# Griffin block on one core: the sums of w_o's blocks and of two of the values' weights made by accumulating DMAs

## The chip, the cores and the metric

The kernel runs on one core of one Trainium2 chip. The metric is the device time of one execution in microseconds (us). All data are float32.

## The reference

One layer of a streaming encoder for 512 rows of width 1024: a norm, one combined projection, two branches (attention over chunks, and a gated recurrence), a merge with two gates, the product with w_o, and a gated feed-forward block.

```python
xn = rmsnorm(x, norm_mix_g)
q, k, v, xr, gr, ga, gb = split(xn @ w_in)
ya = chunked_band_attention(q, k, v, rel_table) @ w_attn_out
hr = rg_lru(causal_depthwise_conv(xr, conv_w, conv_b), ...)
yb = (hr * gelu(gr)) @ w_rnn_out
h = x + (sigmoid(ga + b_a) * ya + sigmoid(gb + b_b) * yb) @ w_o
g, up = split(rmsnorm(h, norm_ffn_g) @ w_ffn_in)
out = rmsnorm(h + (silu(g) * up) @ w_ffn_out, final_norm_g)
```

## The kernel before

**Split products.** Every operand of a large product stands as a high part in the reduced format fp32r and a low part, the rest. ScalarE (ACT) makes the high part with a copy, VectorE (DVE) the low part with a difference (`split`, L84 to L87; in the profile L86 is the high part, L87 the low one). TensorE (PE) then makes three matmuls for each 128 rows of depth (`mm3`, L80 to L82). The tiles of the two parts are called `whl_...`, the loaded weights `raw_...`. Raw weights go through a ring of three buffers of 128x1024 that all stages share, so that a load waits until the tile three loads before it has been split.

**Seven products.** The values (`v_`), the merge with w_o (`o_`) and the feed-forward units (`fg0`, `fu0`, `fg1`, ...) are computed with seven block products in place of eight. Each needs the weight's blocks w11, w21, w22 and four sums of blocks, t1 to t4. On the other side stand sums of the rows' blocks, s1 to s4 (for the values made in `x_sums`, L966). A product of the values or of w_o is 24 matmuls of 512 columns.

**Who makes the sums before.**
- For w_o and for the first feed-forward weights (`f_`), `sums_kept` (L321) loads four blocks of one half of the depth, makes t1 to t4 with four DVE differences of 128x1024, and stores them in DRAM: t1 and t2 of w_o raw, t3 and t4 of w_o already split, as pairs of 1 MB. It runs at the end of the recurrence's loop steps j = 2, 4 (w_o), 6 (f), and once more behind the first key tile (f).
- For the values, `v_weight_sums` (L287) loads three blocks for each half of the depth and makes t1 and t2 with two DVE differences, at j = 3 and 5 of the products with w_rnn_out (`po_yb`), which stand just ahead of the values' products. t3 and t4 are made from t2 as they are needed.
- For w_ffn_out, accumulating DMAs make them: SyncE (SP) copies a block in DRAM (`out_copy`, L222), and later GpSimd (POOL) issues a DMA that adds a second block to it (`out_add`, L226). A small copy to a `cell` makes POOL wait for a given point first. Copies go in each of the 16 heads of the attention, adds behind heads 9, 11, 13 and 15, in the products with w_attn_out (`po_ya`), and in units fg1 and fg2.

**The order.** PE's order is written out by hand from the values on. DVE, ACT, POOL and SP take their instructions in the order that a scheduler found, with some of them kept in the program's order. SP issues nearly all loads, one after the other; an instruction that waits holds up what stands behind it on its engine.

**The merge's stage.** `o_product` (L1222) runs w11, w21, t1, t2, w22, t3, and between the two halves of the second norm, t4. `weights(name, n)` makes ready the weights of the next n products. Behind t3, `norm_half` (L513) transposes the normed rows: a square with a row sum (`hj`), its total (`hsq`), a root (`sd_ffn`), a reciprocal (`rs_ffn`), the scaled rows (`xs_ffn`), then PE's transposes (`pt_ffn`). The feed-forward's first product, w11 of fg0, follows t4.

**The attention.** Each of the 16 heads has its score products on PE, `p` made by DVE and ACT, the scaling of `p` on POOL (L1091), transposes on PE, and the weighted values. In every head POOL also finishes a tile of biases that a DMA brings (L738).

## Time and profile before

| what | value |
|---|---|
| median of 3 runs | 847.2 us (847.09 to 848.59) |
| the profiled execution | 848.82 us |
| its span in the trace | 847.0 us |
| mean granted clock of TensorE | 0.997 |
| DMA traffic | 153.96 MB, mean 182 GB/s |

The span is the time from the first to the last recorded instruction. Times at the start of a row are us from the start of the span; the second number is the time that the row was busy. Brackets at the end of a row hold the idle time ahead of it and what ended that. Matmuls overlap, so PE's pace is read from the starts: at full rate a matmul of 512 columns starts every 0.227 us. The change's places in the span are the recurrence's loop (to about 190 us), the products with w_rnn_out (196 to 242), the values (242 to 282), the attention (282 to 425) and the merge with the start of the feed-forward block (468 to 520).

### The profile page before, as it was taken

The page shows a single profiled execution, that of the slowest core. Times are in us where ns is not written, and L with a number is a line of the kernel's source. Part 1 is how long each engine was busy: PE and PEld are TensorE (multiplying, and loading weights), DVE is VectorE, ACT ScalarE, POOL GpSimd, SP SyncE. Part 2 cuts the span into 40 slices and gives each one's busy share as a digit, 9 for nine tenths or more (in the row PEclk, how much of TensorE's full clock was granted, in tenths as well). Part 3 has the DMA queues.
Part 4 walks back from the last instruction along what each step waited for, and adds up shares of the span by engine and source line. Part 5 has one row for each costly group of instructions (what it writes and reads, how often), then busy time and mean ns, then how long its engine had stood idle before and what let it go on. Part 6 is the DMA issues. An engine that isn't in the chain of part 4 may idle for free.

```text
span 847.0 us, 11664 instructions
## 1 busy us (share of the span) xinstructions
PE 837.2 (99%) x4102; PEld 708.8 (84%) x4102; DVE 654.1 (77%) x960; ACT 524.3 (62%) x868; POOL 159.9 (19%) x207
## 2 busy tenths in 40 slices
PE   9999999999999999999999999999999999999996
PEld 6988888888878888888888888888888999988885
DVE  6667779886999778777568777889777878599784
ACT  7595848773456678878544469663765466555543
POOL 2412030221040043343211000005102322200000
PEclk9999999999999999999999999999999999999998
DMA  8433386687565444549448984555955576455442
GB/s 286 166 103 117 130 298 243 212 271 243 167 205 150 132 134 148 157 152 223 94 132 211 320 294 154 157 187 166 229 176 159 150 187 207 140 177 168 160 165 99
DMA packets 104058, 153.96 MB, mean 182 GB/s; under 512 B 8024, under 2 KB 62896, under 8 KB 103488
## 3 DMA queue, kind: packets, MB, share of 16 engines
q1 hardware_dynamic: 99040, 141.32, 51.2%
q0 software_dynamic: 3728, 8.96, 6.4%
q10 hardware_dynamic: 1232, 2.95, 0.9%
q8 instruction: 32, 0.52, 0.3%
q14 instruction: 26, 0.21, 0.1%
HBM read 139.53 MB, written 30.45 MB: 201 GB/s over the span
## 4 chain that ended last, share of the span: by engine, by line
PE 84%; DVE 7%; ACT 4%; DMA 3%; issue 2%; ACTq 0%; DVEq 0%
PE fu_x L80 2%; PE fu_x L81 2%; PE fu_x L82 2%; PE o L1122 2%; PE fg_x L82 2%; PE fg_x L80 2%; PE fg_x L81 2%; PE pT L1102 2%; PE po_ga L82 2%; PE po_ya L80 2%; PE po_ya L82 2%; PE p_out L81 2%; PE p_out L80 2%; PE po_ya L81 2%; PE p_out L82 2%
## 5 line engine op out<-in xcount | busy, mean ns | idle before, releaser
L1326 POOL TENSOR_TENSOR sg<-sg,keep_fu_x 128x512 f32<-128x512 f32 (+1 forms) x10 | 17.8, 1784 | 163.4 <-DVE keep_fu_x L1325 163.4
L1091 POOL TENSOR_SCALAR p<-p,rl 128x128 f32<-128x128 f32 (+3 forms) x61 | 43.8, 733 | 13.7 <-DVE rl L1087 9.4
L1085 DVE CUSTOM_DVE_ANT_0 p<-s,bias 128x128 f32<-128x128 f32 (+1 forms) x64 | 28.6, 486 | 12.6 <-PE s L1077 11.1
L1086 ACT ACTIVATE p<-p,m 128x128 f32<-128x128 f32 (+1 forms) x64 | 35.5, 555 | 2.3 <-DVE m L1085 2.0
L87 DVE TENSOR_TENSOR whl_fu_w<-raw_fu_w,whl_fu_w 128x1024 fp32r<-128x1024 f32 (+1 forms) x18 | 22.1, 1230 | 9.0 <-ACT whl_fu_w L86 9.0
L87 DVE TENSOR_TENSOR pp<-pT,pp 128x384 fp32r<-128x384 f32 (+1 forms) x48 | 26.9, 595 | 2.0 <-ACT pp L86 1.8
L81 PE MATMUL po_xr<-xnT,whl_xr 128*128 128x512 f32 (+1 forms) x80 | 27.7, 354 | 0.0
L87 DVE TENSOR_TENSOR whl_fu_t<-t_fu,whl_fu_t 128x1024 fp32r<-128x1024 f32 (+1 forms) x18 | 23.2, 1293 | 5.9 <-ACT whl_fu_t L86 5.7
L81 PE MATMUL po_gr<-xnT,whl_gr 128*128 128x512 f32 (+1 forms) x80 | 27.5, 347 | 0.0
L82 PE MATMUL po_gr<-xnT,whl_gr 128*128 128x512 f32 (+1 forms) x80 | 27.3, 347 | 0.0
L82 PE MATMUL po_xr<-xnT,whl_xr 128*128 128x512 f32 (+1 forms) x80 | 27.3, 347 | 0.0
L80 PE MATMUL po_gr<-xnT,whl_gr 128*128 128x512 f32 (+1 forms) x80 | 27.2, 347 | 0.0
L738 POOL MEMSET bias<- 64x64 f32 x16 | 2.5, 155 | 130.7 <-DMA bias<-ext_d 130.7
L80 PE MATMUL po_xr<-xnT,whl_xr 128*128 128x512 f32 (+1 forms) x80 | 26.3, 352 | 0.4 <-ACT xnT L649 0.4
L86 ACT ACTIVATE whl_fu_w<-raw_fu_w 128x1024 fp32r<-128x1024 f32 (+1 forms) x18 | 17.7, 987 | 13.0 <-issue 7.1
L80 PE MATMUL po_k<-xnT,whl_qk 128*128 128x512 f32 x64 | 25.5, 398 | 0.0
L80 PE MATMUL po_q<-xnT,whl_qk 128*128 128x512 f32 x64 | 25.5, 398 | 0.0
L80 PE MATMUL po_ga<-xnT,whl_ga 128*128 128x512 f32 x64 | 25.5, 398 | 0.0
L80 PE MATMUL po_gb<-xnT,whl_gb 128*128 128x512 f32 x64 | 25.3, 395 | 0.0
L86 ACT ACTIVATE whl_fu_t<-t_fu 128x1024 fp32r<-128x1024 f32 (+1 forms) x18 | 17.7, 989 | 12.2 <-PE fu_x L82 8.9
L82 PE MATMUL po_ga<-xnT,whl_ga 128*128 128x512 f32 x64 | 25.1, 392 | 0.1
L81 PE MATMUL po_q<-xnT,whl_qk 128*128 128x512 f32 x64 | 25.0, 390 | 0.0
(610 smaller groups left out, 3036.8 us busy)
## 6 DMA issues: line engine op xcount, KB each, us to landing
raw_qk<-in_w_in_dram SPq DMA_DIRECT2D x32, 256.0 KB, 3.3
out_t<-in_w_ffn_out_dram SPq DMA_DIRECT2D x16, 512.0 KB, 5.5
raw_fu_w<-in_w_ffn_in_dram SPq DMA_DIRECT2D x16, 512.0 KB, 4.7
raw_fo<-in_w_ffn_out_dram SPq DMA_DIRECT2D x14, 512.0 KB, 4.3
raw_t<-out_t SPq DMA_DIRECT2D x24, 256.0 KB, 3.3
raw_xr<-in_w_in_dram SPq DMA_DIRECT2D x8, 512.0 KB, 6.0
raw_gr<-in_w_in_dram SPq DMA_DIRECT2D x8, 512.0 KB, 4.5
raw_ga<-in_w_in_dram SPq DMA_DIRECT2D x8, 512.0 KB, 4.9
```

The costliest lines, as they stand in the source:

```text
L80: pe.matmul(o, sh, mh, start=start, stop=False, skip_group_check=parts)
L81: pe.matmul(o, sh, ml, start=False, stop=False, skip_group_check=parts)
L82: pe.matmul(o, sl, mh, start=False, stop=stop, skip_group_check=parts)
L86: act.activation(hi, src, AF.Copy)
L87: dve.tensor_sub(lo, src, f(hi))
L738: pool.memset(b[64:128, 448:512], NEG)
L1085: dve.tensor_tensor_reduce(prob[qb][:], scs[qb][:, 0:w], bias[:, S - w:S], -1.0, 3e38, ALU.add, ALU.min, nmax[:, qb:qb + 1])
L1086: act.activation(prob[qb][:], prob[qb][:], AF.Exp, bias=nmax[:, qb:qb + 1], scale=-1.0, accum_out=lsum[:, qb:qb + 1])
L1091: eng.tensor_scalar(prob[qb][:], prob[qb][:], rl[:, qb:qb + 1], 1.0, ALU.mult, ALU.mult)
L1102: pe.transpose(pt[:, at * P:(at + 1) * P], prob[qb][:, kb * P:(kb + 1) * P], ident[:])
L1122: pe.matmul(po[:, S - n:S], st, pp[i][:, part, lo:lo + n], start=kb == 0 and part == 0, stop=kb == NT - 1 and part == 1)
L1326: (pool if keep and (unit != f_units[-1] or side) else dve).tensor_mul(o, o, keep[a] if keep else banks[a])
```

## The change

1. t1 to t4 of w_o are made by eight copies in DRAM (SP, heads 0 to 7) and eight accumulating DMAs (POOL, heads 2 to 9). They stand in DRAM raw, so t3 and t4 are now loaded raw (four loads of 512 KB) and split by ACT and DVE, as t1 and t2 were. t3's weights are made ready one product ahead in place of two.
2. `sums_kept` runs for f alone, at j = 2 and 4.
3. t1 and t2 of the values are made by four copies (SP, behind j = 0) and six accumulating DMAs (POOL, four at j = 2 and two at j = 4, every second one behind a `cell`). t1 is loaded through a raw buffer, t2 into the tile that it had.
4. The accumulating DMAs only add, so the signs of some sums change, and with them the signs in `x_sums`, in the merge's row sums and in what is done with the products.
5. The low parts of f's w11 are kept in the program's order (`PINNED`).
6. The copies for w_ffn_out go in heads 8 to 15 and in units fu0 and fg1, their adds behind heads 11, 13, 14, 15, in the products with w_attn_out, and in fu1 and fg2.

```diff
-COPIES = [1] * 16
-ADDS_AT = (9, 11, 13, 15)
-ADDS = {"fg1": 1, "fg2": 1}
+PINNED = (("f", "w11", 0), ("f", "w11", 1))
+COPIES = [0] * 8 + [1] * 8
+ADDS_AT = (11, 13, 14, 15)
+ADDS = {"fu1": 1, "fg2": 1}
...
+    def v_copy(kind, n):
+
+        block = {"t1": (0, 1), "t2": (1, 1), "t3": (1, 1), "t4": (1, 0)}[kind]
+        tc.keep_in_program_order(sp.dma_start(out=v_t[kind, n][:], in_=v_rows(*block, n)))
+
+    def v_add(kind, n, k, after=None):
+
+        if after is not None:
+            cell = cp.tile([P, NT], F32, tag="lsum", bufs=2, name=f"cell_v{kind}{n}_{k.start}")
+            tc.keep_in_program_order(pool.tensor_copy(cell[:, 0:1], after))
+        one = v_t[kind, n][:]
+        two = v_rows(0, int(kind == "t3"), n) if kind in ("t1", "t3") else v_t["t1" if kind == "t2" else "t2", n][:]
+        tc.keep_in_program_order(pool.dma_start(out=one[:, k], in_=two[:, k], accum_op=ALU.add, max_dma_last_dim=4096))
...
-    def v_weight_sums(u):
-
-        b11, b12, b22 = v_raw("t", 0, 0, u), v_raw("t", 0, 1, u), v_raw("t", 1, 1, u)
-        t1, t2 = (aw.tile([P, 2, S], F32, tag="v", bufs=4, name=f"v_t{n}_{u}")[:] for n in (1, 2))
-        dve.tensor_sub(t1, b12, b11)
-        dve.tensor_sub(t2, b22, t1)
...
-            if kind == "t1":
-                src = v_t1[u]
-            elif kind in ("t2", "t4"):
+            if kind in ("t1", "t2"):
+                if kind == "t1":
+                    src = wp.tile([P, 2, S], F32, tag="raw", bufs=3, name=f"raw_v_{kind}_{u}")[:]
+                else:
+                    src = v_t2[u] = aw.tile([P, 2, S], F32, tag="v", bufs=4, name=f"v_t2_{u}")[:]
+                for n in range(2):
+                    sp.dma_start(out=src[:, :, n * CW:(n + 1) * CW], in_=v_t[kind, n][:, 2 * u:2 * u + 2])
+            elif kind == "t4":
                 src = v_t2[u]
...
+    def o_copy(kind, u):
+
+        block = {"t1": (0, 1), "t2": (1, 1), "t3": (1, 1), "t4": (1, 0)}[kind]
+        tc.keep_in_program_order(sp.dma_start(out=o_t[kind, u][:], in_=o_rows_of(*block, u)))
+
+    def o_dma_add(kind, u):
+
+        two = o_rows_of(0, int(kind == "t3"), u) if kind in ("t1", "t3") else o_t["t1" if kind == "t2" else "t2", u][:]
+        tc.keep_in_program_order(pool.dma_start(out=o_t[kind, u][:], in_=two, accum_op=ALU.add, max_dma_last_dim=4096))
...
-            split(hl[u][:, 0], hl[u][:, 1], raw[:])
+                sp.dma_start(out=raw[:], in_=o_t[kind, u][:] if w == "o" else kept_sums[w, int(kind[1])][u].rearrange("p (k e) -> p k e", k=2))
+            act.activation(hl[u][:, 0], raw[:], AF.Copy)
+            ins = dve.tensor_sub(hl[u][:, 1], raw[:], f(hl[u][:, 0]))
+            if (w, kind, u) in PINNED:
+                tc.keep_in_program_order(ins)
...
+                if j < 6:
+                    v_next()
+                    v_next(conv[j + c][2][:, 0:1])
...
+        for what in v_copies[:4] if not j else ():
+            v_copy(*v_copies.pop(0))
         if j:
-            sums_kept(obp, "oof"[j // 2 - 1], (0, 1, 0)[j // 2 - 1])
+            if j < 6:
+                sums_kept(obp, "f", j // 2 - 1)
...
-        if j in (3, 5):
-            v_weight_sums(j // 2 - 1)
...
+            if h < 8:
+                o_copy(*o_copies.pop(0))
             step(copies, COPIES[h])
-            if h in ADDS_AT:
+            if 2 <= h < 10:
+                o_dma_add(*o_adds.pop(0))
+            elif h in ADDS_AT:
                 step(adds)
...
-        w = weights(f"o_{kind}", 2)
+        w = weights(f"o_{kind}", 1 if kind in ("t3",) else 2)
...
+        if unit in f_units[1:3]:
+            step(copies, kind in after)
```

What moves on the engines is shown at three places. Line numbers are those of each kernel's own code.

The first is DVE ahead of the values' products, at the second head's scores (`p`, `m`). Before, the split of w11 (`whl_v_w`), of t1 (`whl_v_t`) and one of the row sums (`v_s`, L981):

```order
L1085 ISA p_2_2171,m_2167<-s_2_2174,bias_2163 128x384
L1085 ISA m_2167 128x1
L87 TENSOR_TENSOR whl_v_w_0_2198<-raw_v_w_000_2200,whl_v_w_0_2198 128x1024
L1085 ISA p_3_2172,m_2167<-s_3_2175,bias_2163 128x512
L1085 ISA m_2167 128x1
L87 TENSOR_TENSOR whl_v_w_1_2199<-raw_v_w_001_2205,whl_v_w_1_2199 128x1024
L981 TENSOR_TENSOR v_s_1897<-v_s_1897,xnT 128x1024
L1152 SCALAR_TENSOR_TENSOR zb_486<-zb_486,po_yb_2197 128x512
L1087 RECIPROCAL rl_2168<-l_2166 128x4
L87 TENSOR_TENSOR whl_v_t_0_2269<-v_t_0_2049,whl_v_t_0_2269 128x1024
```

Now, from a little earlier in the same stretch:

```order
L1032 TENSOR_TENSOR v_s_1877<-v_s_1877,xnT 128x1024
L1201 SCALAR_TENSOR_TENSOR zb_493<-zb_493,po_yb_2055 128x512
L1138 RECIPROCAL rl_2026<-l_2024 128x4
L88 TENSOR_TENSOR v_s4l<-v_s_1877,v_s4h 128x1024
L88 TENSOR_TENSOR whl_v_w_0_2152<-raw_v_w_000_2154,whl_v_w_0_2152 128x1024
L1201 SCALAR_TENSOR_TENSOR zb_493<-zb_493,po_yb_2091 128x512
L1136 ISA p_0_2123,m_2121<-s_01_2127,bias_2117 128x128
L1136 ISA m_2121 128x1
L1136 ISA p_1_2124,m_2121<-s_01_2127,bias_2117 128x256
```

The first half of w11's split and the last row sum have moved ahead of the second head's scores, and t1's split now has a raw tile as its source.

The second is DVE in the merge's stage, from the products with w22 (`o_z`) on. Before:

```order
L1235 SCALAR_TENSOR_TENSOR h_4567<-o_z_4591,h_4567 128x512
L1246 TENSOR_REDUCE hsq_4774<-hsq_0_4585 128x1
L87 TENSOR_TENSOR whl_f_w_0_4778<-raw_f_w_0_4780,whl_f_w_0_4778 128x1024
L1235 SCALAR_TENSOR_TENSOR h_4568<-o_z_4592,h_4568 128x512
L510 RECIPROCAL rs_ffn_4820<-sd_ffn_4818 128x1
L87 TENSOR_TENSOR whl_f_w_1_4779<-raw_f_w_1_4784,whl_f_w_1_4779 128x1024
L519 TENSOR_SCALAR xs_ffn_4822<-h_4567,rs_ffn_4820 128x1024
L1246 TENSOR_REDUCE hsq_4776<-hsq_1_4586 128x1
L1235 SCALAR_TENSOR_TENSOR h_4569<-o_x_4589,h_4569 128x512
L510 RECIPROCAL rs_ffn_4826<-sd_ffn_4824 128x1
L519 TENSOR_SCALAR xs_ffn_4828<-h_4568,rs_ffn_4826 128x1024
```

Now:

```order
L410 TENSOR_TENSOR whl_o_t_0_4720<-raw_o_t_0_4722,whl_o_t_0_4720 128x1024
L1288 SCALAR_TENSOR_TENSOR h_4541<-o_z_4565,h_4541 128x512
L410 TENSOR_TENSOR whl_o_t_1_4721<-raw_o_t_1_4726,whl_o_t_1_4721 128x1024
L1299 TENSOR_REDUCE hsq_4760<-hsq_0_4559 128x1
L1288 SCALAR_TENSOR_TENSOR h_4542<-o_z_4566,h_4542 128x512
L556 RECIPROCAL rs_ffn_4796<-sd_ffn_4794 128x1
L565 TENSOR_SCALAR xs_ffn_4798<-h_4541,rs_ffn_4796 128x1024
L1299 TENSOR_REDUCE hsq_4762<-hsq_1_4560 128x1
L556 RECIPROCAL rs_ffn_4802<-sd_ffn_4800 128x1
L565 TENSOR_SCALAR xs_ffn_4804<-h_4542,rs_ffn_4802 128x1024
L1288 SCALAR_TENSOR_TENSOR h_4543<-o_x_4563,h_4543 128x512
L410 TENSOR_TENSOR whl_f_w_0_4840<-raw_f_w_0_4842,whl_f_w_0_4840 128x1024
```

t4's low parts (`whl_o_t`) have come in around `o_z`; f_w11's low parts have gone from between the two scaled rows to behind the rows `hn` that follow. The row of `whl_f_w` that ends the piece is f_w21's first.

The third is ACT at the same place, from the table load on. Before:

```order
L1265 ACT_TABLE_LOAD
L1265 ACTIVATE warm_150<-eps_t_148 128x1
L1240 ACTIVATE hj0_1_4769,hsq2_0_4585<-h0_4567 128x512
L86 ACTIVATE whl_f_w11_0_4778<-raw_f_w11_0_4780 128x1024
L508 ACTIVATE sd_ffn0_4818<-hsq0_4774,eps_t_148 128x1
L86 ACTIVATE whl_f_w11_1_4779<-raw_f_w11_1_4784 128x1024
L1240 ACTIVATE hj1_1_4772,hsq2_1_4586<-h1_4568 128x512
L508 ACTIVATE sd_ffn1_4824<-hsq1_4776,eps_t_148 128x1
```

Now:

```order
L1318 ACT_TABLE_LOAD
L1318 ACTIVATE warm_158<-eps_t_156 128x1
L409 ACTIVATE whl_o_t3_0_4684<-raw_o_t3_0_4686 128x1024
L409 ACTIVATE whl_o_t3_1_4685<-raw_o_t3_1_4690 128x1024
L409 ACTIVATE whl_o_t4_0_4720<-raw_o_t4_0_4722 128x1024
L409 ACTIVATE whl_o_t4_1_4721<-raw_o_t4_1_4726 128x1024
L1293 ACTIVATE hj0_1_4755,hsq2_0_4559<-h0_4541 128x512
L409 ACTIVATE whl_f_w11_0_4830<-raw_f_w11_0_4832 128x1024
L554 ACTIVATE sd_ffn0_4794<-hsq0_4760,eps_t_156 128x1
L409 ACTIVATE whl_f_w11_1_4831<-raw_f_w11_1_4836 128x1024
L1293 ACTIVATE hj1_1_4758,hsq2_1_4560<-h1_4542 128x512
L554 ACTIVATE sd_ffn1_4800<-hsq1_4762,eps_t_156 128x1
```

Four high parts have come in ahead of the first square; the rest stands as before. On POOL, six accumulating DMAs and three `cell` copies have come into the loop, four of the DMAs between the second `xch` (L764) and the first `a` (L817) of j = 2, and eight DMAs into heads 2 to 9, each behind the scaling of `p`.

More of the change, by code (lines that the diff above doesn't have):

```diff
@@ L275, in out_sums, with v_rows, v_next @@
         return lambda part, k, at=every: hl[:, part, k, at]
-    v_t1, v_t2 = [], []
+    v_t = {(kind, n): dr.tile([P, 4, CW], F32, name=f"v_{kind}_{n}") for kind in ("t1", "t2") for n in range(2)}
+    v_t2 = {}
+    def v_rows(kh, half, n):
+        col = C_V + v_groups[half][n] * CW
+        return w_in[kh * S:kh * S + S, col:col + CW].rearrange("(k p) e -> p k e", p=P)
+    def v_copy(kind, n):
[8 more added lines that the diff above has]
+        tc.keep_in_program_order(pool.dma_start(out=one[:, k], in_=two[:, k], accum_op=ALU.add, max_dma_last_dim=4096))
+    v_copies = [(kind, n) for kind in ("t1", "t2") for n in range(2)]
+    v_adds = [(kind, n, k) for kind in ("t1", "t2") for n in range(2)
+              for k in ((slice(0, 2), slice(2, 4)) if kind in ("t1", "t3") else (slice(0, 4),))]
+    def v_next(after=None):
+        if v_adds:
+            v_add(*v_adds.pop(0), after=after)
     def v_raw(kind, kh, half, u):
@@ L340, in sums_kept, with o_rows_of @@
                 sp.dma_start(out=kept_parts[w, n][u][:, part * D:(part + 1) * D], in_=f(o).rearrange("p k e -> p (k e)"))
+    o_t = {(kind, u): dr.tile([P, 2, S], F32, name=f"o_{kind}_{u}") for kind in ("t1", "t2", "t3", "t4") for u in range(2)}
+    def o_rows_of(kh, half, u):
+        at = kh * S + u * CW
+        return w_o[at:at + CW, half * S:half * S + S].rearrange("(k p) e -> p k e", p=P)
+    def o_copy(kind, u):
[4 more added lines that the diff above has]
+        tc.keep_in_program_order(pool.dma_start(out=o_t[kind, u][:], in_=two, accum_op=ALU.add, max_dma_last_dim=4096))
+    o_sums = [(kind, u) for kind in ("t1", "t2", "t3", "t4") for u in range(2)]
+    o_copies, o_adds = list(o_sums), list(o_sums)
     o_room = []
@@ L983, in x_sums @@
         add, sub = dve.tensor_add, dve.tensor_sub
[L984 removed]
+        chain(s, (sub, x_block(1, 0, 0), x_block(1, 1, 0)), (add, x_block(1, 0, 1)), (sub, x_block(1, 1, 1)))
         parted("s1", s)
@@ L1229, in o_product, with o_add @@
                     start and k == 0, k == 3, parts=True)
-    def o_add(banks, half, cc, last=False):
+    def o_add(banks, half, cc, last=False, by=0.5):
         for a in range(2):
```

31 lines of the change are left out of this document (13 added, 18 removed).

## The prediction

> **What bounds the kernel now.** I read the page first, then TensorE's timeline, then the rows around each stretch that the change touches.
>
> ```profile
> span 847.0 us, 11664 instructions
> PE 837.2 (99%) x4102; PEld 708.8 (84%) x4102; DVE 654.1 (77%) x960; ACT 524.3 (62%) x868; POOL 159.9 (19%) x207
> ```
>
> TensorE (PE) is busy for 99% of the span. The change gives PE the same instructions in the same order, so it can only take away or add places where PE waits. The timeline shows them as starts that come too late:
>
> ```profile
> 217.64 0.22 PE L1076 MATMUL s<-kh,q 128*128 128x128 f32 x1
> ...
> 218.92 0.40 PE L80 MATMUL po_yb<-rnn,whl_yb 128*128 128x512 f32 x1
> ...
> 229.82 0.22 PE L1076 MATMUL s<-kh,q 128*128 128x128 f32 x1
> ...
> 231.59 0.40 PE L80 MATMUL po_yb<-rnn,whl_yb 128*128 128x512 f32 x1
> ...
> 242.50 0.39 PE L80 MATMUL v_x<-whl_v_w,xnT 128*128 128x512 f32 x1
> ...
> 248.56 0.39 PE L80 MATMUL v_z<-whl_v_t,v_s1h 128*128 128x512 f32 x1
> ...
> 251.05 0.50 PE L81 MATMUL v_z<-whl_v_t,v_s1h 128*128 128x512 f32 x1 [0.75 <-DVE whl_v_t L87]
> ...
> 255.04 0.39 PE L80 MATMUL v_x<-whl_v_t,v_s2h 128*128 128x512 f32 x1
> ...
> 260.48 0.39 PE L80 MATMUL v_z<-whl_v_w,v_s4h 128*128 128x512 f32 x1
> ```
>
> These are first matmuls of their steps (251.05, the one with a wait, is inside the second product). Head 0's scores take 218.92 - 217.64 = 1.28 us, head 1's 231.59 - 229.82 = 1.77: 0.49 lost. The values' third product takes 260.48 - 255.04 = 5.44 us (24 matmuls at full rate); the first takes 248.56 - 242.50 = 6.06 (0.62 lost), the second 255.04 - 248.56 = 6.48 (1.04 lost). Together 2.15 us, and VectorE (DVE) is named as the releaser.
>
> **Part 1: the values' t1 and t2.** Why DVE is late there:
>
> ```profile
> 218.37 1.22 DVE L291 TENSOR_TENSOR v_t<-raw_v_t,raw_v_t 128x1024 f32<-128x1024 f32 x1
> ...
> 228.11 0.28 DVE L1085 CUSTOM_DVE_ANT_0 p<-s,bias 128x128 f32<-128x128 f32 x1
> ...
> 236.09 1.23 DVE L292 TENSOR_TENSOR v_t<-raw_v_t,v_t 128x1024 f32<-128x1024 f32 x1
> ...
> 240.45 1.06 ACT L86 ACTIVATE whl_v_w<-raw_v_w 128x1024 fp32r<-128x1024 f32 x1 [8.14 <-DMA raw_v_w<-in_w_in_dram]
> ...
> 222.48 8.79 SPq L283 DMA_DIRECT2D raw_v_t<-in_w_in_dram x6
> ...
> 234.41 9.60 SPq L283 DMA_DIRECT2D raw_v_w<-in_w_in_dram x8
> ```
>
> Removed are four DVE differences of 128x1024 (the first and last are shown; 4 x 1.22 = 4.9 us) and the loads of their blocks, which stand in SyncE's (SP's) queue, waiting for buffers, ahead of the loads of w11. ScalarE (ACT) waits 8.1 us for w11, so its split ends only after PE's 242.50. In the new order the split of w11 stands behind the second scores with none of that ahead of it; its loads can be issued from about 222 on, where the six loads stood, and the split should be ready some 8 us before 242.50. In exchange t1 needs a load into a raw buffer. Its two buffers come free as the last two chunks before it are split; even if that is as late as 240 and 242.5, with the 3.6 us that 256 KB loads of this stage take, 1.06 on ACT and 1.22 on DVE, the halves are ready by 246 and 248.4, ahead of v_z at 248.56 (its second half is needed at 249.9). Head 1's scores wait for DVE's p of head 0 (228.11, over 9 us behind PE's 218.92); DVE now reaches it earlier by the two differences ahead of it, 2.4 us, and by the feed-forward sums that no longer stand behind the first key tile. I take the whole **-2.15 us**; the ends are 0 (DVE is late for another reason) and -2.15.
>
> **Part 2: the merge's weights.** Here PE waits for nothing before the change, and the question is whether it begins to. The rows of DVE, ACT and PE that carry the chain:
>
> ```profile
> 487.47 1.22 DVE L87 TENSOR_TENSOR whl_o_w<-raw_o_w,whl_o_w 128x1024 fp32r<-128x1024 f32 x1
> ...
> 497.47 0.63 ACT L1240 ACTIVATE hj<-h 128x512 f32<-128x512 f32 x1 [0.53 <-DVE h L1235]
> ...
> 499.21 0.15 DVE L1246 TENSOR_REDUCE hsq<-hsq 128x1 f32<-128x2 f32 x1
> ...
> 499.91 1.07 ACT L86 ACTIVATE whl_f_w<-raw_f_w 128x1024 fp32r<-128x1024 f32 x1 [0.22 <-PE o_x L82]
> ...
> 500.06 0.75 DVE L519 TENSOR_SCALAR xs_ffn<-h,rs_ffn 128x1024 f32<-128x1024 f32 x1
> ...
> 501.07 1.03 PE L532 MATMUL pt_ffn<-ident,xs_ffn 128*128 128x128 f32 x8
> ...
> 501.60 1.57 ACT L536 ACTIVATE hn<-pt_ffn,vc 128x256 fp32r<-128x256 f32 x4
> ...
> 502.15 0.68 DVE L1235 SCALAR_TENSOR_TENSOR h<-o_x,h 128x512 f32<-128x512 f32 x1
> ...
> 511.65 0.76 DVE L519 TENSOR_SCALAR xs_ffn<-h,rs_ffn 128x1024 f32<-128x1024 f32 x1
> ...
> 513.78 0.60 PE L532 MATMUL pt_ffn<-ident,xs_ffn 128*128 128x128 f32 x4
> ```
>
> The scaled rows (xs_ffn) end at 500.81, PE transposes them from 501.07: a margin of 0.26 us. For the second half it is 513.78 - 512.41 = 1.4 us. Now t3 and t4 come as four raw loads that need ACT's high part and DVE's low part, and they go through the ring of three raw buffers that also carries the feed-forward's first weights. Each load waits until the tile three loads earlier has been split: t4's first load for w22's second low part, and f_w11's second load for t4's first low part. ACT takes f_w11's second high part ahead of the second root (sd_ffn), so the chain reaches xs_ffn: w22's low part ends 487.47 + 1.22 = 488.7; load L1; high 1.1; low 1.2 and 0.1 of handing over; load L2; high 1.1; square (hj) 0.75 with its accumulator; from hsq to the end of xs_ffn 500.81 - 499.21 = 1.6. That is 494.55 + L1 + L2. The transposes that need it start about 0.2 after 501.07. PE waits s1 = L1 + L2 - 6.7.
>
> What a load takes:
>
> ```profile
> 490.00:495.00 5.00, 5.00 (x24) 4.14 (x23) 1.54 (x3) 1.10 (x3) 0.00 (x0) 1.00 1.03 401
> L319 SPq DMA_DIRECT2D raw_f_w<-in_w_ffn_in_dram x6: 367/383/384, 480.3 to 522.4; - x6
> DMA to landing us min/median/max: 3.8/5.4/6.7
> L365 SPq DMA_DIRECT2D raw_f_t<-f_t x6: 319/320/338, 498.7 to 535.0; - x6
> DMA to landing us min/median/max: 3.3/3.4/4.3
> whl_o_t<-o_hl SPq DMA_DIRECT2D x4, 1024.0 KB, 8.2
> ```
>
> Before, the DMA engines are full at 490 to 495 (share 1.03, 401 GB/s), because four ready pairs of 1 MB are on their way; then 512 KB of f_w takes up to 6.7 us. The change halves the four loads (2 MB less), and the ring now lets only two or three be under way, so I take values near the unloaded ones: L1 = 3.5, L2 = 4.0. The bounds are 3.3 and 5.4 for each. s1 = 0.8 us, between 0 and 4.1. [...]
>
> The second half has a like chain. f_w21's second load waits for the first one's low part, which stands on DVE behind xs_ffn (502.1 with s1) and one h (0.65): low part ended at 504.0. Load L3, high 1.1; behind it in ACT's order hj 0.6, four hn 1.6, hj 0.6, root 0.3, three x 1.2, a kept product 0.5, x 0.4, root 0.3, then on DVE 0.15 and 0.75 with 0.2 of handing over: 6.6. That is 511.7 + L3 against 513.78 + 0.8 + 0.2 = 514.8: s2 = L3 - 3.1. With few loads left under way I take L3 = 3.6: 0.5 us, between 0.2 (3.3) and 2.3 (5.4). Together **+1.3**, between 0.2 and 6.4. A bound below nothing is excluded, since PE waits for nothing here before the change. The pinned low parts of f_w11 stand behind hn's four rows, at 505 to 507.5, and are needed by fg_x behind the transposes at 507.4, the second one half a product (1.4 us) later: nothing.
>
> **Part 3: GpSimd's accumulating DMAs and the loop.**
>
> ```profile
> 78.07 1.30 POOL L764 TENSOR_TENSOR xch<-xc,xch 128x512 fp32r<-128x512 f32 x1 [4.17 <-issue]
> ...
> 92.50 0.62 POOL L817 TENSOR_SCALAR a<-u 128x512 f32<-128x512 f32 x1 [13.13 <-DVE u L815]
> ...
> 94.21 1.63 DVE L87 TENSOR_TENSOR whl_xr<-raw_xr,whl_xr 128x1024 fp32r<-128x1024 f32 x1
> ...
> 105.22 0.39 PE L80 MATMUL po_xr<-xnT,whl_xr 128*128 128x512 f32 x1
> ...
> 387.48 0.15 POOL L738 MEMSET bias<- 64x64 f32 x1 [7.02 <-DMA bias<-ext_d]
> ...
> 391.05 1.28 PE L1102 MATMUL pT<-ident,p 128*128 128x128 f32 x10
> ...
> 419.23 1.05 POOL L233 DMA_DIRECT2D out_t<-in_w_ffn_out_dram  x1 [5.12 <-issue]
> ```
>
> An accumulating DMA keeps GpSimd (POOL) for 1.05 us, and a second one right behind it is held until the first has landed (5.12 us of "issue", a pitch of some 6.1). In the loop at j = 2 four stand between xch (ended 79.4) and a: 79.4 + 3 x 6.1 + 1.05 = 98.8 in place of 92.50. Behind a wait DVE's u and the low part of xr's next weights, 94.21 moved by 6.3: ended 102.1, needed at 105.22. Hidden with 3 us to spare; if a pitch were 7.2 it would not be. The removed o sums relieve DVE behind it, at no gain, since PE doesn't wait there. In the attention eight more accumulating DMAs stand behind the scaling of p in heads 2 to 9, and eight copies of 512 KB share the DMA engines. A head that is even waits on POOL for its bias: at 387.48 it landed, the scaling (about 2.8 us) ended 390.3, transposes 391.05: 0.7 us to spare with one such DMA under way. I take 0; bounds 0 and 4 heads x 1 us. The output's sums, moved by a few heads and units, have tens of us: 0.
>
> **The sum.** -2.15 + 1.3 + 0 = -0.85. The profiled execution took 848.82 us (1.8 outside its span), 1.6 above the median of 847.2; the terms are differences, so I set them on the median: **846.3**. A difference from no change can be told here from about 0.2%, 1.7 us.
>
> **The rivals.**
> 1. *Faster, about 845.3 (0.35).* The gain stays, and the loads land at 3.3 (L1, L2, L3): s1 = 0, s2 = 0.2. For it: the f_t row, and 2 MB less traffic; w22's own loads may land up to 1 us sooner too. Against: the f_w row, whose shortest is 3.8. It decides below s1 + s2 = 0.45.
> 2. *Slower, PE waits for xs_ffn, about 849.4 (0.17).* Loads of 4.7: s1 = 2.7, s2 = 1.6, sum 847.2 - 2.15 + 4.3 = 849.4; at 5.0 it is 850.3. It decides where s1 + s2 passes 3.85, at 4.55 each. For it: the 5.4 us median of f_w and the margin of 0.26 us; against: those loads ran beside the ready pairs.
> 3. *Slower through POOL, about 849.5 (0.06).* The bias lands 1 us later in four even heads and the loop's a delays xr: 846.3 + 3.2.
> 4. *The gain is not there (0.05).* DVE is still late for w11 or t1: 847.2 + 1.3 = 848.5, within 0.2%.
>
> **How the numbers follow.** The forecast's own case, the stall gone and 0.45 to 3.85 us given back, runs from 845.5 to 848.9 and has 0.37. With the fourth rival "same" is 0.42, faster 0.35, slower 0.23. The range takes in rival 1 whole and the greater part of rivals 2 and 3: 844.9 to 849.7.
>
> **What would show it.** Right: v_x and v_z at 5.44 us each and head 1's scores at 1.28; in the merge's stage a PE row of pt_ffn or of the matmul behind it that waits for DVE xs_ffn, by 0.5 to 1 us in each half; raw_f_w landing in 3.5 to 4. Wrong: v_z still waiting for whl_v_t; xs_ffn ahead of PE in both halves (rival 1), or over 2 us behind (rival 2); PE waiting at pT for p in even heads, or at po_xr for whl_xr (rival 3).

## The result, and the profile after

The changed kernel takes 857.0 us (median of 5 runs, 852.9 to 859.3), the kernel before 847.9 (5 runs, 847.1 to 848.6): a ratio of 1.0098, with the 95% interval 1.0074 to 1.0121. It is slower, by 9 us; 846.3 was forecast, and the range ended at 849.7. The profiled execution of the changed kernel took 854.7 us. The head of its page:

```profile
span 852.9 us, 11645 instructions
PE 839.8 (98%) x4102; PEld 709.2 (83%) x4102; DVE 643.8 (75%) x948; ACT 523.5 (61%) x868; POOL 166.3 (20%) x224
```

PE has the same 4102 matmuls and the span is 5.9 us longer. DVE and ACT do less than before, so the cost is waiting. Where it lies comes from the starts of PE's steps, put side by side for the two profiled executions: the values' stage gains 2.17 us; the loop loses 4.05, the attention 0.54, the merge's stage 0.77, the feed-forward 2.9 (and 0.2 come back at the very end). This execution was 2.3 us faster than the median of its kernel, so the profile shows less than the 9 us. PE's waits in the changed kernel (in total, times, longest):

```profile
PE fg_x L82 <- DVE whl_fg_w L88: 1.3, 1, 1.3
...
PE rg L839 <- POOL xch L810: 0.9, 2, 0.7
PE rg L839 <- ACT xch L809: 0.7, 1, 0.7
PE fu_x L82 <- DVE whl_fu_t L88: 0.7, 2, 0.4
...
PE o_z L83 <- DVE ms L88: 0.5, 1, 0.5
```

The forecast wait (xs_ffn) is not among them; waits in the loop and the feed-forward, which were forecast at nothing, head the list. (Left out are three waits of the first 25 us, which the kernel before has too.)

**The values' stage** did what the forecast said. First matmuls of the values' four products:

```profile
246.03 0.39 PE L81 MATMUL v_x<-whl_v_w,xnT 128*128 128x512 f32 x1
...
251.47 0.39 PE L81 MATMUL v_z<-whl_v_t,v_s1h 128*128 128x512 f32 x1
...
256.92 0.39 PE L81 MATMUL v_x<-whl_v_t,v_s2h 128*128 128x512 f32 x1
...
262.36 0.39 PE L81 MATMUL v_z<-whl_v_w,v_s4h 128*128 128x512 f32 x1
```

The first three take 5.44, 5.45 and 5.44 us, and the second head's scores 1.27: no place is left where PE starts late.

**The loop** is where the largest loss begins. POOL at j = 2, then ACT behind it:

```profile
80.33 1.27 POOL L297 DMA_DIRECT2D v_t<-in_w_in_dram  x1
...
85.50 1.16 POOL L297 DMA_DIRECT2D v_t<-in_w_in_dram  x1 [3.68 <-issue]
91.47 1.14 POOL L297 DMA_DIRECT2D v_t<-in_w_in_dram  x1 [4.81 <-issue]
...
96.31 1.14 POOL L297 DMA_DIRECT2D v_t<-in_w_in_dram  x1 [3.51 <-issue]
97.04 1.67 POOL L863 TENSOR_SCALAR a<-u 128x512 f32<-128x512 f32 x2
```

```profile
101.03 1.07 ACT L889 ACTIVATE u<-u 128x1024 f32<-128x1024 f32 x1 [3.54 <-DVE u L865]
...
110.53 1.06 ACT L362 ACTIVATE f_b<-f_b 128x1024 fp32r<-128x1024 f32 x1 [5.49 <-DMA f_t<-f_b]
112.06 1.05 ACT L87 ACTIVATE whl_gr<-raw_gr 128x1024 fp32r<-128x1024 f32 x1
...
121.96 1.06 ACT L87 ACTIVATE whl_gb<-raw_gb 128x1024 fp32r<-128x1024 f32 x1 [4.06 <-DMA raw_gb<-in_w_in_dram]
```

The first `a` starts at 97.04 instead of 92.50. ACT's root `u` waits 3.54 us for it (through DVE), DVE's sums f_b, which stand where the kernel before has those of o, start behind that at 102.05 instead of 97.50, and ACT's high part f_b, which overwrites t2's tile and so needs its store f_t out of the way, waits 5.49 us. (Before, the same wait for o was 0.81.) Behind the waiting f_b ACT has the second half of gr's split, which frees a raw buffer, and with it the later loads; it starts at 112.06, where the kernel before had it at 107.36. gb's second split comes at 121.96, where the kernel before had it at 116.30. A lag of about 5 us is carried through the recurrence to j = 6, and there PE pays. First before (the 12 gate products `rg` and the next step), then after:

```profile
161.53 1.66 PE L793 MATMUL rg<-xch,wrg 64*128 64x512 f32 x12
163.12 0.50 PE L80 MATMUL po_gb<-xnT,whl_gb 128*128 128x512 f32 x1
```

```profile
162.00 0.97 PE L839 MATMUL rg<-xch,wrg 64*128 64x512 f32 x6
163.69 0.73 PE L839 MATMUL rg<-xch,wrg 64*128 64x512 f32 x4 [0.72 <-ACT xch L809]
165.11 0.49 PE L839 MATMUL rg<-xch,wrg 64*128 64x512 f32 x2 [0.68 <-POOL xch L810]
165.53 0.67 PE L81 MATMUL po_gb<-xnT,whl_gb 128*128 128x512 f32 x1
166.00 0.63 PE L82 MATMUL po_gb<-xnT,whl_gb 128*128 128x512 f32 x1
...
168.98 0.46 PE L83 MATMUL po_gb<-xnT,whl_gb 128*128 128x512 f32 x1
```

The two waits cost 1.4 us, 1.94 with the breaks around them. Then matmuls that follow each other at 0.23 us elsewhere follow at 0.43 until 169: another 1.64 us. (0.47 was already lost at j = 4.) The windows of the changed kernel show why (busy us and instructions of PE, PEld, DVE, ACT, POOL; the granted clock; the DMA share; GB/s):

```profile
162.00:165.50 3.50, 2.10 (x13) 0.97 (x12) 1.56 (x3) 2.47 (x4) 1.29 (x1) 1.00 0.50 144
165.50:169.00 3.50, 3.50 (x11) 2.70 (x10) 2.65 (x4) 3.50 (x5) 0.00 (x0) 0.53 0.00 0
169.00:173.00 4.00, 4.00 (x19) 3.28 (x18) 2.35 (x3) 3.90 (x7) 0.00 (x0) 0.99 0.84 186
```

After a stretch of 3.5 us in which PE was busy for 2.1, the granted clock falls to 0.53 for 3.5 us, and in the 4 us behind that it is 0.99. Ahead of the fall PE was thin and broken, not idle all along: 13 matmuls in the 3.5 us, with waits of 0.72 and 0.68.

**The feed-forward.** DVE's sum for the first unit waits for its load, and in fg_x a weight comes late:

```profile
650.60 1.23 DVE L453 TENSOR_TENSOR t_fu<-raw_fu_w,t_fu 128x1024 f32<-128x1024 f32 x1 [2.47 <-DMA raw_fu_w<-in_w_ffn_in_dram]
...
673.41 0.44 PE L82 MATMUL fg_x<-whl_fg_w,hn 128*128 128x384 f32 x1 [1.30 <-DVE whl_fg_w L88]
```

The kernel before had that sum at 645.66 with 0.79 of waiting; 3.2 us of the difference come from earlier stages, 1.7 are new. Four of the output's accumulating DMAs now lie at 636 to 662, in unit fu1, where there were none.

**The attention.** The time from the bias's issue to its landing, in the view of its tile:

```profile
DMA to landing us min/median/max: 4.1/6.1/7.3
```

In the kernel before the same row has 3.1/4.1/5.9. The median is 2 us later. PE lost little by it in this execution (0.54 us), but more in others, as the experiments show.

### The profile page after: what moved, and what is told of

The parts are those of the page before. It is cut to its first block, busy times and chain, and to the rows that moved or that the text cites. A ratio compares the mean times of both kernels' runs of the same rounds, so it can differ in the third digit from the quotient of the medians.

```text
span 852.9 us, 11645 instructions
## 1 busy us (share of the span) xinstructions
PE 839.8 (98%) x4102; PEld 709.2 (83%) x4102; DVE 643.8 (75%) x948; ACT 523.5 (61%) x868; POOL 166.3 (20%) x224
## 4 chain that ended last, share of the span: by engine, by line
PE 85%; DVE 5%; DMA 4%; issue 3%; ACT 2%; POOL 0%; ACTq 0%; SPq 0%; DVEq 0%; POOLq 0%
PE fg_x L82 2%; PE fg_x L83 2%; PE fg_x L81 2%; PE o L1173 2%; PE pT L1153 2%; PE po_ga L83 2%; PE po_q L81 2%; PE po_q L82 2%; PE po_ya L83 2%; PE po_q L83 2%; PE po_ya L81 2%; PE po_ya L82 2%; PE p_out L82 2%; PE p_out L81 2%; PE po_yb L83 2%
## 5 line engine op out<-in xcount | busy, mean ns | idle before, releaser
L1142 POOL TENSOR_SCALAR p<-p,rl 128x128 f32<-128x128 f32 (+3 forms) x61 | 35.0, 588 | 41.4 <-DVE rl L1138 37.1
L88 DVE TENSOR_TENSOR whl_fu_t<-t_fu,whl_fu_t 128x1024 fp32r<-128x1024 f32 (+1 forms) x18 | 26.3, 1466 | 3.7 <-ACT whl_fu_t L87 3.5
L81 PE MATMUL po_gb<-xnT,whl_gb 128*128 128x512 f32 x64 | 25.9, 405 | 0.0
L82 PE MATMUL po_gb<-xnT,whl_gb 128*128 128x512 f32 x64 | 25.7, 401 | 0.0
L83 PE MATMUL po_gb<-xnT,whl_gb 128*128 128x512 f32 x64 | 25.5, 398 | 0.0
L81 PE MATMUL po_q<-xnT,whl_qk 128*128 128x512 f32 x64 | 25.5, 398 | 0.0
L81 PE MATMUL po_ga<-xnT,whl_ga 128*128 128x512 f32 x64 | 25.4, 397 | 0.0
```

The costliest lines, as they stand in the source:

```text
L81: pe.matmul(o, sh, mh, start=start, stop=False, skip_group_check=parts)
L82: pe.matmul(o, sh, ml, start=False, stop=False, skip_group_check=parts)
L83: pe.matmul(o, sl, mh, start=False, stop=stop, skip_group_check=parts)
L88: dve.tensor_sub(lo, src, f(hi))
L1142: eng.tensor_scalar(prob[qb][:], prob[qb][:], rl[:, qb:qb + 1], 1.0, ALU.mult, ALU.mult)
```

## The experiments

Three losses had to be told apart, and each had a rival. **Loop:** POOL held at j = 2 is enough by itself, or only with the f sums that stand behind it. **Attention:** the bias's late landing makes PE wait, or the added DMAs do it in some other way. **Output's sums:** their move into fu1 costs, or the feed-forward's loss is the loop's lag handed down. Besides: is the gain of 2.15 us real, and whose is it? Each run is compared with runs of the kernel before on the same chip, and the chip differs from one group of runs to the next, so ratios compare better than medians. The ratios are given with their 95% intervals, and losses by stage are from one profiled execution against the first of before unless another is named.

**e1: two v adds a step.** Each of j = 2, 4 and 6 issues two of the six accumulating DMAs, where the change has four at j = 2 and two at j = 4.

```diff
-                if j < 6:
-                    v_next()
-                    v_next(conv[j + c][2][:, 0:1])
+                v_next()
```

> The changed kernel with the values' six accumulating DMAs placed two in each of the steps j = 2, 4 and 6, directly behind the two xch, in place of four at j = 2 and two at j = 4; no cell copies. Theory H (four accumulating DMAs hold GpSimd ahead of a at j = 2, the recurrence falls behind by 4.5 us and TensorE waits at rg of j = 4 and 6): a of j = 2 starts at about 92.5 again, the matmuls of po_gb behind rg of j = 6 and of po_q come 3 to 4 us earlier than in the changed kernel (po_q at 174 to 175 in place of 178.2), and the time falls by 3 to 4 us, to about 853.5. Theory S (the feed-forward sums moved to j = 4 make ScalarE wait for a store and hold up the recurrence): rg of j = 6 stays late, po_q stays at 176 or more, and the time falls by 0 to 1 us.

852.9 us, 1.005 [1.0032, 1.0067]. `a` is at 92.44 and the loop loses nothing, so the four adds in POOL's order at j = 2 are needed for that loss. But 5 us remain: the attention loses 2.7, the merge 1.6, the feed-forward 2.6. POOL and PE at one head:

```profile
351.60 0.15 POOL L784 MEMSET bias<- 64x64 f32 x1 [6.96 <-DVE m L1134]
351.85 3.65 POOL L1140 TENSOR_SCALAR p<-p,rl 128x128 f32<-128x128 f32 x4
```

```profile
354.88 0.33 PE L1151 MATMUL pT<-ident,p 128*128 128x128 f32 x1 [1.75 <-POOL p L1140]
```

The memset of the bias's corner stands in POOL's order ahead of the scaling of p, and waits for the bias; it is the bias of the head two further on. (The profile names DVE's m, the release of the bias's buffer; the load stands in between.) The load takes 5.7 us to its landing in the median here and 4.1 before; the delay goes to the scaling, and PE waits 1.75 us at pT.

**e2: the f sums back.** The feed-forward's sums stand where the kernel before had them, so that nothing is summed at j = 2 and 4; the v adds stay four a step.

```diff
-            if j < 6:
-                sums_kept(obp, "f", j // 2 - 1)
+            if j == 6:
+                sums_kept(obp, "f", 0)
...
     k_tile(0)
+    sums_kept(obp, "f", 1)
```

> The changed kernel with the two feed-forward sums where they were before, at j = 6 and behind the first key tile, so that the steps j = 2 and 4 hold no sums at all. Theory S: the 2.9 us wait of ScalarE ahead of f_b's high part at j = 4 is gone, rg of j = 6 no longer waits, and the time falls by 2 to 4 us, to 853 to 855. Theory H: a of j = 2 stays at 97, xch of j = 4 stays 5 us late, and the time falls by 0 to 1.5 us.

850.0 us, 1.0021 [1.0005, 1.0037]. The decisive pair of rows: `a` is still late, and PE's `rg` at j = 6 waits for nothing.

```profile
96.67 1.67 POOL L863 TENSOR_SCALAR a<-u 128x512 f32<-128x512 f32 x2
```

```profile
161.12 1.66 PE L839 MATMUL rg<-xch,wrg 64*128 64x512 f32 x12
```

So POOL's delay is hidden by itself; the loop pays for it only where sums, with their wait for a store on ACT, stand behind it. By the ratios e2 takes back 0.77%, 6.5 us, where 2 to 4 were expected and the loop's loss is 4; what else it takes back no run separates. Its own profile still loses 4.0 us in the attention, 1.2 in the merge and 0.8 in the feed-forward.

**e3: the output's sums back** at their old heads and units, but for the four adds behind heads, which stay behind 11, 13, 14 and 15.

```diff
-COPIES = [0] * 8 + [1] * 8
+COPIES = [1] * 16
-ADDS = {"fu1": 1, "fg2": 1}
+ADDS = {"fg1": 1, "fg2": 1}
```

> The changed kernel with the copies and the last adds for w_ffn_out where they were before: 16 copies in the attention's 16 heads, adds in fg1 and fg2. Theory C (the accumulating DMAs in unit fu1 make raw_fu_w land late there, VectorE falls behind, TensorE waits for whl_fu_t and whl_fg_w): the waits at 655, 673 and perhaps 723 us (0.7, 1.6, 0.6 us in the changed kernel) are gone and the time falls by 2 to 3 us, to about 854.5. Rival (those waits are chance, or belong to GpSimd's own work): it falls by less than 1 us. The 16 copies beside the eight of w_o could add a wait in the attention, where there was 0.4 us.

854.4 us, 1.0067 [1.0052, 1.0082]. The feed-forward's losses are gone; the loop loses 4.0. The mean granted clock of its profile is 0.996, against 0.995 in the changed kernel and 0.999 in e1, whose loop loses nothing.

**e4: the values' t1 and t2 by DVE in the loop**, as before the change, with adds in place of the differences; no v DMAs.

```diff
+        if j in (3, 5):
+            v_weight_sums(j // 2 - 1)
```

> The changed kernel with the values' t1 and t2 made by VectorE again, in the products with w_rnn_out as before, with additions in place of differences (the signs stay those of the changed kernel); no copies and no accumulating DMAs for them. Theory H: the loop's 4 us are gone (a at 92.5), and the 2.2 us that the values' stage gained are lost too: 857.0 - 4.0 + 2.2 = about 855. Theory S: the loop's loss stays, and the time rises by 1 to 2 us, to about 858.5.

851.4 us, 1.0041 [1.0025, 1.0058]. The loop loses nothing, as in e1. But v_x and v_z take 5.44 us here too, with the four DVE passes back in place, where a loss of 2.2 was expected: the stall can be absent without the v DMAs.

**e5: the values' part alone**, two adds a step, on the kernel before (diff as in the change, for v only).

> The kernel before with the values' part alone: t1 and t2 by copies and accumulating DMAs, two in each of j = 2, 4, 6 behind xch as in the run that moved them; the sums of w_o and of the feed-forward block, and all sums for w_ffn_out, as before. Theory (the losses belong to the loop's crowded GpSimd, to w_o's DMAs in the attention and to w_ffn_out's in fu1): the values' stage gains its 2.2 us and nothing is lost, about 845.8 us. Rival (any accumulating DMA beside the loop's sums costs TensorE something): rg of j = 4 or 6 waits and the time is 847 or more.

847.2 us, 0.9989 [0.9975, 1.0002]: no measurable difference, though its profile has no stall and lies 2.3 us ahead of the first profile of before.

**e6: the merge's part alone**: the changed kernel with the edits of e2, e3 and e4.

> The changed kernel with the values' sums on VectorE, the feed-forward sums at j = 6 and behind the first key tile, and w_ffn_out's copies and adds as before (but for the heads of four adds): what is left of the change is w_o's part. Theory (w_o's DMAs in heads 0 to 9 delay the bias, GpSimd scales p late, and the merge's loads delay xs_ffn): TensorE waits at pT in even heads by 2 to 3 us and at pt_ffn by about 1 us, no gain in the values' stage, about 851 us. Rival (those waits came from the values' part or from chance): 848 us, with the waits of before.

852.0 us, 1.0043 [1.0028, 1.0059]. The attention loses 2.6 us and the merge 1.9; loop and feed-forward nothing. The values' stage has no stall here either, with no v DMAs in the kernel. The merge's wait is the forecast one, by its name:

```profile
503.48 0.87 PE L582 MATMUL pt_ffn<-ident,xs_ffn 128*128 128x128 f32 x6 [1.27 <-DVE xs_ffn L569]
```

**e8: e1 and e3 together**, which leaves the attention and the merge as the change has them.

> The changed kernel with the values' adds two a step and w_ffn_out's copies and adds as before. The loop's 4 us and the feed-forward's 2.9 us are both gone; what is left is the gain of 2.2, the attention's 0.4 to 4 and the merge's 1 to 1.6: about 849.5 us. Rival (the two causes are one, and each run's loss moves elsewhere): 852 or more.

854.0 us, 1.0067 [1.0044, 1.009], no better than e1 or e3 alone: the rival's time, not the 849.5 of the theory. Its loop loses nothing, but its profile loses 5.1 us in the attention, 1.6 in the merge and 0.9 in the feed-forward. Part of the 5.1 is the clock again. Behind the wait for POOL's p in head 6 it falls for one more stretch (columns as above):

```profile
334.40:337.90 3.50, 1.28 (x8) 0.74 (x6) 3.18 (x7) 2.91 (x7) 3.11 (x5) 0.99 1.06 265
337.90:341.40 3.50, 3.25 (x12) 2.70 (x12) 1.81 (x5) 2.39 (x6) 2.59 (x5) 0.52 0.90 282
```

e2 and e7 have such a fall in the attention too, to 0.52 and 0.51.

**e7: e8 with a third bias buffer**, so that the load might start earlier.

```diff
-        b = aw.tile([P, S], F32, tag="bias", bufs=2, name=f"bias{h}")
+        b = aw.tile([P, S], F32, tag="bias", bufs=3, name=f"bias{h}")
```

> The next kernel (two a step, w_ffn_out's sums back) with three buffers for the bias in place of two, so that a bias can be asked for a head earlier. Theory (the bias's DMA lands late in even heads because w_o's copies and adds share the DMA engines): the waits at pT are gone and the time is 2 to 3 us below the next kernel's, about 847. Rival (GpSimd is held by the adds themselves): no difference.

852.7 us, 1.0064 [1.0043, 1.0085]: a miss, and PE's waits at pT stay. The loads do start a head earlier: three biases, in place of two, are asked for ahead of the heads. But the memset moves up with its load. In head 6 POOL waits ahead of the scaling of p as before, now for a bias three heads on (7.91 us; 8.20 in e8):

```profile
333.52 0.15 POOL L784 MEMSET bias<- 64x64 f32 x1 [7.91 <-DMA bias<-ext_d]
```

So the number of buffers was not the limit. It says nothing against the theory, and leaves the place of the memset as what can be changed.

**e10: e8 with the bias loaded around its corner.** The memset comes first and two DMAs fill the rest, so POOL never waits for a load.

```diff
-        sp.dma_start(out=b[:], in_=band)
         pool.memset(b[64:128, 448:512], NEG)
+        sp.dma_start(out=b[0:64, :], in_=bass.AP(tensor=src.tensor, offset=src.offset, ap=[[1, 64], [1, S]]))
+        sp.dma_start(out=b[64:128, 0:448], in_=bass.AP(tensor=src.tensor, offset=src.offset + 64, ap=[[1, 64], [1, 448]]))
```

> The kernel of the run with two adds a step and w_ffn_out's sums back (854.0 us), in which the bias is loaded by two DMAs around the masked corner, so that GpSimd's memset of the corner no longer waits for the DMA. Theory (in the attention TensorE waits because the memset stands in GpSimd's order ahead of the scaling of p and waits for a bias that lands 1 to 3 us later than before): the waits at pT are gone, about 849 to 850 us. Rival (GpSimd is late by the adds' own issue or by slower p): the waits at pT stay, 853 or more.

847.8 us, 0.9995 [0.9982, 1.0008]. The first entry of what ended the idle time ahead of pT (us in total, times), in e8:

```profile
  POOL p L1140: 5.9, 8
```

and in e10:

```profile
  ACT pp L87: 1.9, 9
```

The row for POOL's p, which counts PE and its weight loads together, is gone, and with it 6.2 us of the median (0.72% by the ratios). The two parts of the bias also land sooner than the whole did, 4.0 us in the median against 6.1 in e8, but POOL's memset now stands ahead of them and waits for neither. The merge still waits:

```profile
501.17 0.88 PE L578 MATMUL pt_ffn<-ident,xs_ffn 128*128 128x128 f32 x6 [1.61 <-DVE xs_ffn L565]
```

**e11: e10 with two raw buffers of their own for t4**, which cuts the ring that ties t4's loads to f_w11's.

```diff
-            raw = wp.tile([P, 2, S], F32, tag="raw", bufs=3, name=f"raw_{w}_{kind}_{u}")
+            own = w == "o" and kind == "t4"
+            raw = (o_room[0] if own else wp).tile([P, 2, S], F32, tag="raw4" if own else "raw", bufs=2 if own else 3, name=f"raw_{w}_{kind}_{u}")
```

> The run before it with two raw buffers of their own for t4 of w_o, so that the ring of three no longer holds up the feed-forward's first weights. Theory (the chain of loads through the ring makes xs_ffn late): TensorE no longer waits at pt_ffn, 1 to 1.5 us less than the run before it, about 848.5. Rival (the loads are late because the DMA engines are full): the wait stays, no difference.

846.9 us, 0.9992 [0.9976, 1.0007]. The eight transposes run in one piece, and PE no longer waits in the merge:

```profile
499.01 1.04 PE L579 MATMUL pt_ffn<-ident,xs_ffn 128*128 128x128 f32 x8
```

In the medians the step from e10 is not clear of the intervals. This is the best of the versions that keep the whole change, and it does not measurably beat the kernel before.

**e9 and e12: the kernel before and the changed kernel profiled once more**, to see what of the first profiles is one execution's.

> The kernel before, unchanged, profiled a second time. If the 2.2 us that TensorE lost in the values' stage belong to every execution, the second trace shows the same three starts (scores of head 1 at 1.77 us, v_x 6.06, v_z 6.48). If they belong to the first profiled execution, which was 1.6 us above the median, the second trace shows less of them, and the run of the values' part alone could gain no more than it did (0.8 us in the median).

> The changed kernel, unchanged, profiled a second time. Theory: its losses sit in the same four places (rg in the loop, pT in even heads, the merge, the feed-forward units), and their sizes in the attention and in the feed-forward units change from execution to execution, since they hang on when DMAs land; the loop's loss stays at 3 to 4 us. Rival: the loop's loss is absent in a second execution, and was chance.

e9 took 847.4 us. Its values' products:

```profile
241.98 0.39 PE L80 MATMUL v_x<-whl_v_w,xnT 128*128 128x512 f32 x1
...
247.43 0.39 PE L80 MATMUL v_z<-whl_v_t,v_s1h 128*128 128x512 f32 x1
...
253.12 0.39 PE L80 MATMUL v_x<-whl_v_t,v_s2h 128*128 128x512 f32 x1
...
258.56 0.39 PE L80 MATMUL v_z<-whl_v_w,v_s4h 128*128 128x512 f32 x1
```

5.45, 5.69, 5.44: of the 2.15 us only 0.25 is left, in the same kernel. ACT's first split of w11 is at 238.50 here and was at 240.45 in the first profile, after the same long wait for the load (7.59 and 8.14 us): the load came 2 us later in the first. What made it late stays open. In the merge, at o_z, this second profile of before loses 0.35 us against the first, so up to that much of the losses there needs no change at all. e12 took 852.2 us, with the loop losing 0.9 (one wait, and behind it matmuls that start every 0.23 us), the attention 1.7, the merge 1.0, the feed-forward 2.3:

```profile
163.51 0.51 PE L839 MATMUL rg<-xch,wrg 64*128 64x512 f32 x2 [0.58 <-POOL xch L810]
...
502.50 0.88 PE L578 MATMUL pt_ffn<-ident,xs_ffn 128*128 128x128 f32 x6 [0.42 <-DVE xs_ffn L565]
```

The four losses come back in a second execution, in other sizes; the loop's was expected to stay at 3 to 4 us. The delay that reaches j = 6 is smaller in e12: POOL's last xch, at 159.04 in the first profile of before, is at 162.18 here and was at 163.77. So 3.1 us of delay cost PE 0.9, and 4.7 cost 4.0, the fall of the clock and the 0.47 at j = 4 included.

**e13, e14, e15: one loss at a time.** Each is e11 with one part put back as the change has it: the loop's four adds a step (e13), the bias by one DMA (e14), the output's sums (e15); the diffs are those of e1, e10 and e3, reversed.

> The mended kernel (846.9 us: two adds a step, w_ffn_out's sums back, bias around the corner, own raw buffers for t4) with the values' adds as in the change, four at j = 2 and two at j = 4. Theory (GpSimd held at j = 2, VectorE's sums behind it): TensorE waits at rg of j = 6 and the time rises by 1 to 4 us, to 848 to 851. Rival (the loop's wait comes only with the others): 847.

> The mended kernel with the bias loaded by one DMA again, so that GpSimd's memset waits for it. Theory: the waits at pT are back and the time rises by 5 to 6 us, to about 852.5, as the run without this mend was 6.2 us above the run with it. Rival (that difference belonged in part to the ring): 849 or less.

> The mended kernel with w_ffn_out's copies and adds where the change puts them (copies in heads 8 to 15, fu0, fg1; adds in fu1 and fg2). Theory (accumulating DMAs beside fu1's loads): TensorE waits at whl_fu_t or whl_fg_w, and the time rises by 2 to 3 us, to 849 to 850. Rival: 847.

| kernel | median us | ratio to before | added to e11 |
| --- | --- | --- | --- |
| e11 | 846.9 | 0.9992 [0.9976, 1.0007] | |
| e13, loop | 851.2 | 1.0034 [1.0016, 1.0052] | 0.42% |
| e14, bias | 851.0 | 1.0027 [1.0012, 1.0043] | 0.35% |
| e15, output's sums | 848.5 | 1.0007 [0.9987, 1.0028] | 0.15% |
| e10, t4 in the ring | 847.8 | 0.9995 [0.9982, 1.0008] | 0.03% |

The last column is the difference of the ratios. It sums to 0.95%, against 1.06% between the changed kernel and e11. e13 and e14 stand clear of e11's interval; the other two do not, so for them the cost is not shown in the medians, only as waits in the profiles. e14's 0.35%, 3 us, is less than the 6.2 between e8 and e10: the expected 5 to 6 did not come, so the parts are not wholly independent, or the two groups of runs differ by that much. The profiles show one difference. e14 has the same waits for POOL's p as e8 (5.9 us, 8 times) and a stretch just as thin, and yet the clock stays up (1.00, where e8 has 0.52), which leaves its attention at 3.8 us of loss against 5.1:

```profile
334.40:337.90 3.50, 1.23 (x6) 0.51 (x4) 3.19 (x7) 2.68 (x7) 3.25 (x5) 1.00 1.02 271
337.90:341.40 3.50, 3.21 (x18) 2.78 (x19) 1.90 (x5) 2.76 (x7) 3.03 (x7) 1.00 0.91 308
```

e13 has the waits and the fall of the clock (0.58 at 165.50 to 169.00) as the changed kernel has them:

```profile
163.71 0.73 PE L840 MATMUL rg<-xch,wrg 64*128 64x512 f32 x4 [0.93 <-ACT xch L810]
165.12 0.80 PE L840 MATMUL rg<-xch,wrg 64*128 64x512 f32 x2 [0.68 <-POOL xch L811]
...
166.44 0.63 PE L82 MATMUL po_gb<-xnT,whl_gb 128*128 128x512 f32 x1
```

e15 has the feed-forward's wait by itself, with a loop that is on time, so there it is not handed down from the loop. (It cannot be all: e8 and e7, with these sums back, still lose 0.9 and 2.0 us in the feed-forward.)

```profile
667.86 0.44 PE L82 MATMUL fg_x<-whl_fg_w,hn 128*128 128x384 f32 x1 [1.30 <-DVE whl_fg_w L88]
```

## Why the prediction was wrong

- **Part 1 (-2.15): right in the trace, wrong as a term of the median.** v_x, v_z and the scores run as forecast. The step that failed is "the terms are differences, so I set them on the median". The stall was a property of the one execution that was profiled, 1.6 us above its median; the second profile of before has 0.25 of it. The part that the median can lose is smaller: e5, the values' part alone, measures -0.11% [-0.25, +0.02], about 0.9 us, with 2.15 at the edge of the interval. The cause that was given, DVE's four differences and their loads, is not enough by itself either: the second profile of before has all of them and 0.25 of the stall, and e4 and e6 keep four such passes and have none. What stays open is whether the stall shows in a share of the executions of before; of two profiles of that kernel one has it, of the fifteen of kernels with some part of the change none.
- **Part 2 (+1.3): the mechanism right, its size only roughly.** PE does wait for xs_ffn, through t4's loads in the ring of raw buffers: 0.4 us in e12, 1.3 to 1.6 in e6 and e10 (0.8 was forecast for the first half), and in the profile of e11 cutting the ring takes it away. The 0.5 of the second half did not come in these (0.2 and less there, and made up for at once). In the medians the ring is worth 0.9 us (e10 against e11), by the ratios 0.3, and neither is clear of noise. In the first profile of the changed kernel PE lost its 0.77 us earlier in that stage, mostly at o_z for ms, and the chain then had slack.
- **Part 3 (0): here the prediction failed, in three places.** *The loop:* `a` was forecast at 98.8 and came at 97.04, so the pitch of these four DMAs was well taken, if a little long (6.1; they start 5.2, 6.0 and 4.8 us apart); "hidden with 3 us to spare" looked only at the next consumer, whl_xr, and held there. The step that failed is "the removed o sums relieve DVE behind it": the f sums have taken their place at j = 2 and 4, and only what stood at j = 6 and behind the first key tile is gone. So sums still stand behind `a`, with a store that ACT's high part waits for, and that wait (5.49 us) holds gr's split and the loads behind it. The delay and the sums behind it are both needed (e1 and e4 take away the one, e2 the other, and none loses anything in the loop). *The attention:* "0.7 us to spare" was read rightly and then taken as enough (the bias that POOL waits for is that of the head two further on, not the head's own); the landing moved by 2 us, more than the margin. It was the third rival in kind, given a chance of 0.06. *The output's sums:* "tens of us" was the distance to their own consumers. What they collide with is other work's loads: DVE's sum waits 2.47 us for raw_fu_w, 0.79 before, and 2.40 in e15. In the medians this loss is not clear of noise.
- **The sum.** Each margin was weighed against one delay alone, with everything else as before. The third rival named the bias and the loop's `a`, the latter by another consumer, and put 3.2 us on them; from the forecast to the measured time it is 10.7, of which 0.7 is the base (the kernel before took 847.9 us in the runs of the result, and 847.2 was used). The parts that were put back singly account for 0.95% of the 1.06% between e11 and the changed kernel. No profile of the changed kernel shows the whole: both were taken in executions below its median (854.7 and 852.2 against 857.0).

## What to carry to other kernels

A step that is late on one engine can be called hidden only when everything behind it was followed: here POOL's `a`, 4.5 us late, spared its next consumer and reached PE through ACT's wait of 5.49 us. Ask first what waits for something else behind that step. That the results of background DMAs are due late does not make them free: look for the smallest margin among the loads that run beside them, here the bias's 0.7 us, against a landing 2 us later. And a stall is worth taking away only if a second execution of the same kernel has it: compare the profiled time with the median before a term is set on it.

## What was not expected of the hardware

- The granted clock fell without PE being idle all along: 3.5 us with PE busy 60%, with thin matmuls (64x512) and two waits, were followed by 3.5 us at 0.53, at a price of 1.64 us, more than either of the waits ahead of it (0.72 and 0.68). Behind the one wait of 0.58 us in e12 the matmuls start every 0.23 us, as elsewhere. The busy share alone does not decide it: in the attention the clock fell to 0.52 in e8 behind a stretch with PE busy for 1.28 of 3.5 us, and stayed at 1.00 in e14 behind one with 1.23, at the same place. What does decide it was not measured.
- GpSimd's accumulating DMAs that add a block of a weight to a copy in DRAM followed each other at 4.8 to 6.0 us (80.33, 85.50, 91.47, 96.31 in the loop), each 0.3 to 0.4 us behind the landing of the one before (85.24, 91.12, 95.91: 4.9, 5.6 and 4.4 us after the issue); other work of POOL, the `cell` copies at 81.62 and 92.17, ran in between, only the next DMA was held. It was not so for all: the two at j = 4 that add one of the kernel's own DRAM tiles to another start 2.1 us apart (128.59 and 130.67) and land 5.3 and 6.8 us after their issues, and in e1 both stand in 1.72 us (from 159.17). Why they differ was not tried.
- Beside w_o's DMAs the bias, a load of 256 KB, landed later: 4.1 us after its issue in the median before and in e5, which has no DMAs for w_o in the attention, 6.1 in the changed kernel and 5.5 in e12.
